# Other rates for the conditioning loads, three more steps before the transposes of the convolution rows, and a later request of norm rows in a two-layer decoder trunk

## The chip, the cores and the metric

The kernel runs on one core of one Trainium2 chip. The metric is device time in microseconds (us) of one execution, as the median of several runs. A core has five engines that work side by side, each through its own queue in order: TensorE (PE, matmuls and transposes), VectorE (DVE), ScalarE (ACT), GpSimd (POOL), and SyncE (SP), which here only issues DMA transfers. An instruction waits in its queue until what it needs is done, and everything behind it in that queue waits too.

## The reference

Two layers, one sequence of 256 tokens of width 2048. Each layer has a token mixer (forgetting attention in the first, sliding-window attention in the second) and a gated ConvFFN of inner width 5632. Every sub-layer is wrapped by a modulation and a norm whose six vectors come from the conditioning vector c:

```
c_act = jax.nn.silu(c)
for i in range(DEPTH):
    mod = c_act @ ada_w[i] + ada_b[i]
    sh1, sc1, g1, sh2, sc2, g2 = jnp.split(mod[:, None, :], 6, axis=-1)
    h = x * (1.0 + sc1) + sh1
    y = mixer(h)
    x = layer_norm(DEEPNORM_ALPHA * x + (1.0 + g1) * y, ln_mix_g[i], ln_mix_b[i])
    h = x * (1.0 + sc2) + sh2
    y = conv_ffn(h, ffn_w_up[i], ffn_conv_w[i], ffn_conv_b[i], ffn_w_down[i])
    x = layer_norm(DEEPNORM_ALPHA * x + (1.0 + g2) * y, ln_ffn_g[i], ln_ffn_b[i])
return x
```

All weights are f32. `ada_w` alone is two matrices of 2048 x 12288.

## The kernel before

**Weights and steps.** Every projection streams its weight in tiles of 256 rows by 512 columns (0.524 MB). `stream` asks for a tile on SP's queue (L261), ACT rounds it to a high part `wh` (L264), DVE subtracts to get the low part `wl` (L275), and PE multiplies high by high, high by low and low by high, so that the product has nearly the precision of f32. Four buffers each hold `wh` and `wl`; ten hold the loaded tiles. One consumed weight tile is one **step**: after it, `tick` runs some of the background work. The tokens are held on PE in the down and output projections (sums `xs`), the weights in the up projections (sums `ws`).

**Conditioning.** A vector (l, v) of `mod` (l the layer, v from 0 to 5: shift, scale, gate of the mixer, then of the ConvFFN) is a sum over 2048 rows of `ada_w`. `ada_vector` loads it in 32 tiles of 0.524 MB (L387, `wa`), and DVE adds each one, times an element of silu(c), to an accumulator `acc` (L393; the first by L391). There is one accumulator. For a shift or scale, PE then turns it in 16 transposes (L431), ACT sums the columns (L435) and DVE adds the bias (L417); a gate goes through four matmuls with ones (L403), after its bias came by a load on POOL's queue (L381). The vectors come in the order of `ada_list` (L363). How fast: each step adds `rate` to a debt, and each whole unit of debt runs one piece, mostly one load with its product (`ada_tick`, L461). When a scale (l, 4) is done, the generator holds until the next norm (L440). If a vector is needed and not there, `ada_need` (L467) runs the missing pieces at once. The rates are set stage by stage with numbers written into the program.

**Norms between sub-layers.** `between` (L1143) stands between two sub-layers: it asks for shift and scale, lets PE spin on a few dummy matmuls, normalises (`normalise`, L647 on ACT for the first 128 tokens, L649 on DVE for the others), transposes x on PE (L488) and applies the merged scale and shift (L681 to L683, then `mod_pair`, L498 to L503). x itself is still to be multiplied by the norm's weights for the next residual. That is background work: `affine` loads four tiles of norm rows on SP (L656) and runs two DVE operations for each of eight blocks of x (L667, L668), one block a step.

**Other background work.** `columns` (L142) turns the convolution weights from rows into columns: POOL requests the rows (L162, L163), a step later PE transposes them (L167), another step later DVE copies them to `ccol` (L169). It does this for both layers, one after the other. The rows take one of four buffers that are shared with sums of query and key parts and other short-lived tiles. In the second mixer `pair` runs the softmax of two heads over several steps.

**Order.** The engines' order comes from a scheduler that may move instructions past each other where data allow it, except those pinned to the program's order (`pin(..., True)`), among them the products L393 and the operations of `affine`. So a change of one number can move neighbours too.

Of the kernel before, what the change touches and what calls it, by code (L numbers as in the profile page):

```python
# [41 lines left out]
def hybrid_trunk(ctx: ExitStack, tc: tile.TileContext, a: dict, out: bass.AP):  # L42
# [99 lines left out]
    def columns():  # L142

        r = ttile("rows").rearrange("p (a b) -> p a b", b=P)
        for l in range(1, DEPTH):
            nc.gpsimd.dma_start(r[:NADA, l, :], adab[l])
        for q, nm in enumerate(("ln_mix_g", "ln_mix_b", "ln_ffn_g", "ln_ffn_b")):
            nc.gpsimd.dma_start(r[q * 32:(q + 1) * 32, 0, :], a[nm].rearrange("l (r p) -> (l r) p", p=P))
        yield
        for l in range(1, DEPTH):  # L150
            pt = bank()
            nc.tensor.transpose(pt[:, :NADA], r[:NADA, l, :], ident[:NADA, :NADA])
            yield
            nc.vector.tensor_copy(acol[:, l, :], pt[:, :NADA])
        pt = bank()
        nc.tensor.transpose(pt[:, :P], r[:, 0, :], ident)
        yield
        nc.vector.tensor_copy(lcol.rearrange("p a b c -> p (a b c)"), pt[:, :P])
        for l in range(DEPTH):
            r = ttile("rows").rearrange("p (a b) -> p a b", b=P)  # L160
            for j in range(CW):
                nc.gpsimd.dma_start(r[:NF, j, :], a["ffn_conv_w"][l, j].rearrange("(r p) -> r p", p=P))  # L162
            nc.gpsimd.dma_start(r[:NF, CW, :], a["ffn_conv_b"][l].rearrange("(r p) -> r p", p=P))  # L163
            yield
            pt = bank()
            for j in range(CW + 1):
                nc.tensor.transpose(pt[:, j * NF:(j + 1) * NF], r[:NF, j, :], ident[:NF, :NF])  # L167
            yield
            nc.vector.tensor_copy(ccol[:, l].rearrange("p a b -> p (a b)"), pt[:, :(CW + 1) * NF])  # L169
# [165 lines left out]
    def later(gens, lag=1):  # L335

        bg["wait"].extend((g, lag) for g in gens)
# [313 lines left out]
    def ln_rows(name, l):  # L651
        gb, bb = [], []
        for c in range(0, D, D // 2):
            for b, nm in ((gb, "_g"), (bb, "_b")):
                w = wtile("ln")
                nc.sync.dma_start(w.rearrange("p a f -> p (a f)"), a[name + nm][l, c:c + D // 2].partition_broadcast(P))  # L656
                b += [w[:, 0, :], w[:, 1, :]]
        return gb, bb

    def affine(name, l):  # L660

        gb, bb = ln_rows(name, l)
        yield
        for d in range(D // 512):
            c = slice(d * 512, (d + 1) * 512)
            for t in range(NT):
                pin(nc.vector.scalar_tensor_tensor(x[:, t, c], x[:, t, c], ALPHA, gb[d], op0=ALU.mult, op1=ALU.mult))  # L667
                pin(nc.vector.scalar_tensor_tensor(x[:, t, c], bb[d], ALPHA, x[:, t, c], op0=ALU.mult, op1=ALU.add))  # L668
                yield
# [70 lines left out]
    def out_proj(oT, full, w_o, l):  # L740
        def stat(kc, t):
            while kc not in full:
                step()
            return oT[kc][0][:, t * P:(t + 1) * P], oT[kc][1][:, t * P:(t + 1) * P]

        ps = {d: x_banks() for d in range(2)}

        def part(d, ks):
            use = x_mm_end(ps[d], stat, KC, 2) if d == D // WB - 1 else                 lambda kc, h, l_: x_mm(ps[d], kc, h, l_, stat, KC - 1)
            stream(w_o, 0, d * WB, ks, use)  # L750

        for i, ks in enumerate((range(0, 8), range(8, 12))):
            then(lambda i=i: ada.update(rate=(1.3, 0.3)[l]))
            for d in range(2):
                part(d, list(ks))
        then(lambda: (ada_need(l, 2), ada.update(rate=(1.3, 0.6)[l])))
        for d in range(D // WB):
            if d < 2:
                part(d, list(range(12, KC)))
            else:  # L760
                ps[d] = x_banks()
                part(d, list(range(KC)))
            then(lambda d=d: defer(residual(ps[d], d, gates[l, 2], True)), d == D // WB - 1)
        then(lambda: (flush(), ada.update(gate_free=True)), True)
# [204 lines left out]
    def swa(l, j):  # L969
# [94 lines left out]
        ps = x_stationary(w_in, KOFF, 0, KC, hstat)  # L1064
        for t in range(NT):
            then(lambda t=t, ps=ps: defer(evac_kv(t, ps[t])))
        then(lambda: (ada.update(rate=0.8), bg.update(gap=2)))
        for g in range(SKV):
            if g == 1:
                then(lambda: ada.update(rate=0.3))  # L1070
            ps = x_stationary(w_in, g * WB, 0, KC, hstat)
            then(lambda g=g, ps=ps: defer(evac_q(g, ps)))
        out_proj(oT, full, w_o, l)
# [2 lines left out]
    def conv_ffn(l):  # L1076
        w_up, w_dn = a["ffn_w_up"][l], a["ffn_w_down"][l]
        NB = DFF // WB
        cw = lambda j, f: ccol[:, l, j, f:f + 1]

        def conv(pf, f):
            u = tp.tile([P, S], F32, tag="u", bufs=3, name="u")
            nc.scalar.activation(u, pf, AF.Identity, bias=cw(CW, f), scale=cw(2, f))  # L1083
            nc.vector.scalar_tensor_tensor(u[:, 1:], pf[:, :S - 1], cw(1, f), u[:, 1:],  # L1084
                                           op0=ALU.mult, op1=ALU.add)
            nc.vector.scalar_tensor_tensor(u[:, 2:], pf[:, :S - 2], cw(0, f), u[:, 2:],  # L1086
                                           op0=ALU.mult, op1=ALU.add)
            return u

        def evac(ps, f0, then):  # L1090
            u = None
            for f in range(5):
                v = conv(ps[f // 2][:, f % 2, :], f0 + f) if f < 4 else None
                if u is not None:
                    then(f - 1, u)
                u = v
                yield
                yield

        def silu(sil):  # L1100
            def f_(f, u):
                nc.scalar.activation(sil[f // 2][:, (f % 2) * S:(f % 2 + 1) * S], u, AF.Silu)
            return f_

        def gated(sil, gT):
            def f_(f, u):
                nc.vector.tensor_tensor(u, u, sil[f // 2][:, (f % 2) * S:(f % 2 + 1) * S], op=ALU.mult)
                g = gtile("gT")
                split(g[:, 0, :], g[:, 1, :], u)
                gT.append(g)  # L1110
            return f_

        sbs = [(0, 6), (6, NB)]
        for si, (b0, b1) in enumerate(sbs):
            gT = []
            then(lambda: ada.update(rate=(0.64, 0.4)[l]))
            for b in range(b0, b1):
                ps = w_stationary(w_up, b * WB)
                sil = [ttile("sil") for _ in range(2)]
                then(lambda ps=ps, b=b, sil=sil: defer(evac(ps, b * 4, silu(sil))))  # L1120
                ps = w_stationary(w_up, DFF + b * WB)
                then(lambda ps=ps, b=b, sil=sil, gT=gT: defer(evac(ps, DFF // P + b * 4, gated(sil, gT))))

            def stat(kc, t, gT=gT):
                while kc >= len(gT):
                    run_post()
                return gT[kc][:, 0, t * P:(t + 1) * P], gT[kc][:, 1, t * P:(t + 1) * P]

            def ready(si=si):
                if si == 0:  # L1130
                    drain()
                ada_need(l, 5)
                ada["rate"] = (0.85, 0.4)[l]

            then(ready)
            for d in range(D // WB):
                ps = x_stationary(w_dn, d * WB, b0 * 4, (b1 - b0) * 4, stat, (2, 4)[l] if si > 0 and d == D // WB - 1 else 0)
                then(lambda ps=ps, d=d, si=si: defer(residual(ps, d, gates[l, 5], si == len(sbs) - 1)),
                     si > 0 and d == D // WB - 1)
        then(lambda: (flush(), ada.update(gate_free=True)), True)  # L1140


    def between(l, v, g, b, name, ll):  # L1143

        ada_need(l, v)
        ada_need(l, v + 1)
        place(20 if v else 56)
        o = bank("spin")
        release()
        spin(o, 3)  # L1150
        modulate(*merged(l, v, g, b, ll), normalise, o)
        behind[0] = 2
        later([affine(name, ll)])

    for l in range(DEPTH):
        if l > 0:
            then(lambda l=l: (between(l, 0, 2, 3, "ln_ffn", l - 1), ada.update(rate=.3)), True)
            swa(l, l // 2)
        else:
            fox(l, l // 2)  # L1160
        then(lambda l=l: between(l, 3, 0, 1, "ln_mix", l), True)
        conv_ffn(l)
# [36 lines left out]
```

## Time and profile before

| what | us |
|---|---|
| median of 3 runs | 2226.65 |
| lowest and highest of them | 2225.01 and 2227.9 |
| the profiled execution, its own time | 2226.14 |
| its span from the first to the last instruction | 2224.4 |
| PE busy within the span | 2168.7 |
| DVE busy | 1785.4 |
| ACT busy | 1152.5 |

In the profile's rows a group of instructions stands as: line, engine, operation, output<-inputs, size, count; then busy time, mean of one in ns, and idle time of the engine just before, with what ended it. In the timeline a row begins with the start in us from the span's beginning and the duration; brackets hold the idle time before it and what was waited for. `PEld` is PE's weight load, which runs beside its matmuls. In the view by windows each row is a stretch of time with its length, then each engine's busy time with the number of instructions, the granted share of PE's clock, the share of time the DMA engines were busy, and GB/s.

### The profile page before, as it was taken

The numbers are of one execution on the slowest core, as the hardware profiler recorded it, in microseconds if no ns is written. First come the engines' busy times: TensorE is split into PE (matmuls) and PEld (weight loads), VectorE is DVE, ScalarE is ACT, GpSimd is POOL, SyncE is SP. The second block draws the span as 40 slices with busy tenths as digits, with TensorE's granted clock in tenths as the row PEclk, the third lists the DMA queues.
The fourth block names the chain that finished last, engine by engine and source line by source line (L and its number), as shares of the span: only waits on it lengthen the run. The fifth ranks groups of instructions, "written<-read, shape, count | busy, mean of one in ns | idle before, by whom it ended". The sixth has DMA issues, their size and how long they took to land. (4 is left out here: it accounts for less than half of the span.)

```text
span 2224.4 us, 38328 instructions
## 1 busy us (share of the span) xinstructions
PE 2168.7 (97%) x14915; PEld 1973.9 (89%) x14915; DVE 1785.4 (80%) x2442; ACT 1152.5 (52%) x1825; POOL 19.9 (1%) x48
## 2 busy tenths in 40 slices
PE   6999999999999999999999999989999999999997
PEld 5999888889999888999987777779999888999986
DVE  6978999979979978798799877789888555666756
ACT  3435655555555543555634577555555533555532
POOL 0000000000000000000000000000000000000000
PEclk9999999999999999999999999999999999999998
DMA  9999999969979989799798755678888566666563
GB/s 337 382 359 345 348 358 321 330 222 331 345 250 313 327 300 348 263 307 320 251 344 304 257 181 163 208 272 291 281 270 267 183 195 191 198 191 197 192 194 109
DMA packets 274246, 602.98 MB, mean 271 GB/s; under 512 B 21062, under 2 KB 29960, under 8 KB 273552
## 3 DMA queue, kind: packets, MB, share of 16 engines
q1 hardware_dynamic: 273008, 595.85, 78.9%
q0 software_dynamic: 1056, 4.69, 0.6%
q8 instruction: 116, 1.90, 0.3%
q14 instruction: 66, 0.54, 0.1%
HBM read 598.37 MB, written 2.10 MB: 270 GB/s over the span
## 5 line engine op out<-in xcount | busy, mean ns | idle before, releaser
L264 ACT CAST wh<-w 128x1024 fp32r<-128x1024 f32 x728 | 765.4, 1053 | 810.1 <-PE ws L75 272.9
L275 DVE TENSOR_TENSOR wl<-w,wh 128x1024 fp32r<-128x1024 f32 x728 | 887.5, 1222 | 338.5 <-ACT wh L264 322.4
L75 PE MATMUL ws<-hH,wh 128*128 128x256 f32 x6656 | 1153.2, 278 | 4.6 <-ACT hH L84 2.1
L75 PEld LDWEIGHTS ws<-hH,wh 128*128 128x128 f32 x6656 | 1009.4, 189 | 12.5 <-issue 3.6
L75 PE MATMUL ws<-hH,wl 128*128 128x256 f32 x3328 | 916.5, 277 | 3.4 <-DVE wl L275 3.2
L75 PEld LDWEIGHTS ws<-hH,wl 128*128 128x128 f32 x3328 | 626.4, 189 | 4.9 <-DVE wl L275 4.8
L75 PE MATMUL xs<-wh,gT 128*128 128x512 f32 x1408 | 435.5, 389 | 0.0
L75 PEld LDWEIGHTS xs<-wh,gT 128*128 128x128 f32 x1408 | 264.3, 188 | 54.6
L75 PE MATMUL xs<-wl,gT 128*128 128x512 f32 x704 | 273.9, 389 | 0.0
L75 PE MATMUL xs<-wh,hH 128*128 128x512 f32 x704 | 236.8, 403 | 0.3 <-ACT wh L264 0.2
L393 DVE SCALAR_TENSOR_TENSOR acc<-wa,cact,acc 128x1024 f32<-128x1024 f32 x180 | 228.0, 1277 | 0.0
L393 DVE SCALAR_TENSOR_TENSOR acc<-wa,cactp,acc 128x1024 f32<-128x1024 f32 x128 | 162.4, 1277 | 0.0
L75 PEld LDWEIGHTS xs<-wh,hH 128*128 128x128 f32 x704 | 131.3, 189 | 29.9 <-issue 0.9
L75 PEld LDWEIGHTS xs<-wl,gT 128*128 128x128 f32 x704 | 132.2, 188 | 27.4
L75 PE MATMUL xs<-wl,hH 128*128 128x512 f32 x352 | 139.1, 396 | 2.2 <-DVE wl L275 2.2
L1083 ACT ACTIVATE u<-ws,ccol 128x256 f32<-128x256 f32 x176 | 96.7, 562 | 58.7 <-PE ws L75 44.4
L75 PE MATMUL xs<-wh,oT 128*128 128x512 f32 x384 | 124.9, 395 | 0.0
L1084 DVE SCALAR_TENSOR_TENSOR u<-ws,ccol,u 128x255 f32<-128x255 f32 x176 | 82.5, 477 | 18.0 <-ACT u L1083 17.8
L75 PEld LDWEIGHTS xs<-wh,oT 128*128 128x128 f32 x384 | 72.0, 188 | 15.8 <-DVE oT L85 0.3
L1086 DVE SCALAR_TENSOR_TENSOR u<-ws,ccol,u 128x254 f32<-128x254 f32 x176 | 83.0, 477 | 2.1
L75 PEld LDWEIGHTS xs<-wl,hH 128*128 128x128 f32 x352 | 66.5, 189 | 18.1 <-DVE wl L275 4.5
L568 DVE SCALAR_TENSOR_TENSOR oacc<-wo,cact,oacc 128x1024 f32<-128x1024 f32 (+1 forms) x68 | 73.4, 1079 | 8.6 <-DMA wo<-in_ada_w_dram 7.4
(215 smaller groups left out, 1265.9 us busy)
## 6 DMA issues: line engine op xcount, KB each, us to landing
w<-in_ffn_w_up_dram SPq DMA_DIRECT2D x352, 512.0 KB, 4.8
wa<-in_ada_w_dram SPq DMA_DIRECT2D x320, 512.0 KB, 5.7
w<-in_ffn_w_down_dram SPq DMA_DIRECT2D x176, 512.0 KB, 4.8
w<-in_fox_w_in_dram SPq DMA_DIRECT2D x96, 512.0 KB, 7.0
wo<-in_ada_w_dram SPq DMA_DIRECT2D x48, 512.0 KB, 9.4
w<-in_swa_w_in_dram SPq DMA_DIRECT2D x40, 512.0 KB, 4.7
w<-in_fox_w_o_dram SPq DMA_DIRECT2D x32, 512.0 KB, 6.3
w<-in_swa_w_o_dram SPq DMA_DIRECT2D x32, 512.0 KB, 4.4
```

The source lines that it names most:

```text
L75: return nc.tensor.matmul(o, lhsT, rhs, start=start, stop=stop, **kw)
L264: pin(nc.scalar.copy(h, w), False)
L275: pin(nc.vector.tensor_tensor(l, w, f32(h), op=ALU.subtract), behind[0] > 0)
L393: pin(nc.vector.scalar_tensor_tensor(ac, wo, (cactp if row else cact)[:, k:k + 1], ac, op0=ALU.mult, op1=ALU.add), True)
L568: nc.vector.scalar_tensor_tensor(acc, w[:, k], cact[:, kc:kc + 1], acc, op0=ALU.mult, op1=ALU.add)
L1083: nc.scalar.activation(u, pf, AF.Identity, bias=cw(CW, f), scale=cw(2, f))
L1084: nc.vector.scalar_tensor_tensor(u[:, 1:], pf[:, :S - 1], cw(1, f), u[:, 1:], op0=ALU.mult, op1=ALU.add)
L1086: nc.vector.scalar_tensor_tensor(u[:, 2:], pf[:, :S - 2], cw(0, f), u[:, 2:], op0=ALU.mult, op1=ALU.add)
```

## The change

It changes three things:

- conditioning rates: first ConvFFN, down projections 0.85 to 0.95; second layer: first norm and key/value projection 0.3 to 0.2, first query block 0.8 to 0.6, other query blocks 0.3 to 0.65, output projection 0.3 to 0.65 and from the third part on 0.6 to 0.75
- the background generator `columns` makes four yields in place of one between the request of the convolution rows and their transposes
- `affine` takes a delay in steps: 7 at the norm between the layers, 0 at the norms inside a layer, as before

Nothing is computed otherwise, and the loads, products and matmuls are as many as before. Lines behind the two insertions have numbers higher by 1 (from 165 on) or by 3 (from 662 on).

```
@@ -161,7 +161,8 @@
             for j in range(CW):
                 nc.gpsimd.dma_start(r[:NF, j, :], a["ffn_conv_w"][l, j].rearrange("(r p) -> r p", p=P))
             nc.gpsimd.dma_start(r[:NF, CW, :], a["ffn_conv_b"][l].rearrange("(r p) -> r p", p=P))
-            yield
+            for _ in range(4):
+                yield
             pt = bank()
@@ -657,8 +658,10 @@
-    def affine(name, l):
-
+    def affine(name, l, delay):
+
+        for _ in range(delay):
+            yield
         gb, bb = ln_rows(name, l)
         yield
@@ -750,10 +753,10 @@
-            then(lambda i=i: ada.update(rate=(1.3, 0.3)[l]))
+            then(lambda i=i: ada.update(rate=(1.3, 0.65)[l]))
             for d in range(2):
                 part(d, list(ks))
-        then(lambda: (ada_need(l, 2), ada.update(rate=(1.3, 0.6)[l])))
+        then(lambda: (ada_need(l, 2), ada.update(rate=(1.3, 0.75)[l])))
@@ -1064,10 +1067,10 @@
-        then(lambda: (ada.update(rate=0.8), bg.update(gap=2)))
+        then(lambda: (ada.update(rate=0.6), bg.update(gap=2)))
         for g in range(SKV):
             if g == 1:
-                then(lambda: ada.update(rate=0.3))
+                then(lambda: ada.update(rate=0.65))
@@ -1130,7 +1133,7 @@
-                ada["rate"] = (0.85, 0.4)[l]
+                ada["rate"] = (0.95, 0.4)[l]
@@ -1150,11 +1153,11 @@
-        later([affine(name, ll)])
+        later([affine(name, ll, 0 if v else 7)])
...
-            then(lambda l=l: (between(l, 0, 2, 3, "ln_ffn", l - 1), ada.update(rate=.3)), True)
+            then(lambda l=l: (between(l, 0, 2, 3, "ln_ffn", l - 1), ada.update(rate=.2)), True)
```

The numbers say little about where instructions now stand, so three places of the built order follow.

The first is DVE's queue at the last inner norm, between the second mixer and the second ConvFFN: the end of the last residual (L631 to L636), then the norm. Before:

```order
L631 BN_STATS stats<-x 128x6
L634 BN_AGGR mv<-stats 128x2
L636 TENSOR_SCALAR mv<-mv 128x1
L393 SCALAR_TENSOR_TENSOR acc<-wa,cact,acc 128x1024 x5
L649 TENSOR_SCALAR x<-x,mv,rs 128x512 x4
L417 SCALAR_TENSOR_TENSOR cv<-tot,acol 128x16
L681 TENSOR_TENSOR G<-cv,lcol 128x16
L682 TENSOR_TENSOR B<-cv,lcol 128x16
L683 TENSOR_TENSOR B<-B,cv 128x16
L499 TENSOR_SCALAR t<-sm,G,B 128x256 x2
```

After the change the same place reads:

```order
L632 BN_STATS stats<-x 128x6
L635 BN_AGGR mv<-stats 128x2
L637 TENSOR_SCALAR mv<-mv 128x1
L650 TENSOR_SCALAR x<-x,mv,rs 128x512 x4
L500 TENSOR_SCALAR t<-sm,G,B 128x256 x2
L501 TENSOR_TENSOR hH<-t,hH 128x256 x2
```

The five products of vector (1,4) and the four small operations that make its merged columns have left this place for the output projection ahead of it.

The second is PE's queue at the same norm, from the last matmuls of the output projection to the first transposes of x. Before:

```order
L75 MATMUL xs<-wh,hH 128x512 x2
L75 MATMUL xs<-wl,hH 128x512
L75 MATMUL xs<-wh,hH 128x512
L431 MATMUL sm<-ident,acc 128x128 x16
L75 MATMUL spin<-mask,ident 128x384 x3
L488 MATMUL sm<-ident,x 128x128 x8
```

With the change, where the second of four groups of such transposes stands inside the output projection (its sums go over oT and hH, the attention's result):

```order
L75 MATMUL xs<-wh,hH 128x512 x2
L75 MATMUL xs<-wl,hH 128x512
L75 MATMUL xs<-wh,hH 128x512
L432 MATMUL sm<-ident,acc 128x128 x4
L75 MATMUL xs<-wh,oT 128x512
L75 MATMUL xs<-wl,oT 128x512
```

The 16 transposes of the accumulator no longer stand between the mixer and the norm; they come in fours, between weight tiles.

The third is PE's queue in the first mixer, where the convolution rows of the first layer are turned (L167, L168 after; S is a head's scores). Before:

```order
L75 MATMUL ws<-hH,wh 128x256 x2
L75 MATMUL ws<-hH,wl 128x256
L167 MATMUL sm<-ident,rows 128x88 x3
L75 MATMUL ws<-hH,wh 128x256
L167 MATMUL sm<-ident,rows 128x88
```

After:

```order
L75 MATMUL ws<-hH,wh 128x256 x2
L75 MATMUL ws<-hH,wl 128x256
L168 MATMUL sm<-ident,rows 128x88 x4
L75 MATMUL S<-Bm,A 128x128
L75 MATMUL S<-qh 128x128
L75 MATMUL S<-ql,qh 128x128
```

They stand 88 matmuls further back and in one piece, ahead of a head's scores.

## The prediction

> **What bounds the kernel now.** I read the page's busy table first, then the waits of TensorE, then the three norms between sub-layers in the view by windows, and last the timeline of the one norm that stands out.
>
> ```profile
> span 2224.4 us, 38328 instructions
> PE 2168.7 (97%) x14915; PEld 1973.9 (89%) x14915; DVE 1785.4 (80%) x2442; ACT 1152.5 (52%) x1825; POOL 19.9 (1%) x48
> ```
>
> TensorE (PE) is busy for 2168.7 of 2224.4 us, so at most 55.7 us of the span are gaps. No rate changes the number of its matmuls. The change can only move gaps, so the question is which gaps it touches. The next view shows three stretches, each from the last matmul of one sub-layer to the first of the next; columns are busy time of PE, weight loads, VectorE (DVE), ScalarE (ACT), GpSimd (POOL), then granted clock, DMA share and GB/s.
>
> ```profile
> 470.46:476.28 5.82, 4.47 (x20) 2.65 (x19) 4.85 (x13) 4.47 (x8) 1.12 (x2) 1.00 0.00 0
> 1208.68:1214.51 5.83, 4.49 (x21) 2.65 (x19) 4.93 (x13) 4.52 (x8) 1.11 (x2) 1.00 0.21 84
> 1468.54:1484.98 16.44, 8.93 (x36) 6.62 (x35) 12.10 (x23) 10.49 (x42) 2.58 (x3) 0.69 0.64 228
> ```
>
> The first two norms take 5.82 and 5.83 us. The third, the last inner norm, takes 16.44 us, and there the granted clock is 0.69 instead of 1.00. The timeline says why:
>
> ```profile
> 1468.54 0.39 PE L75 MATMUL xs<-wh,hH 128*128 128x512 f32 x1
> 1476.44 3.67 PE L431 MATMUL sm<-ident,acc 128*128 128x128 f32 x16 [7.51 <-DVE acc L393]
> 1479.90 3.37 PE L75 MATMUL spin<-mask,ident 128*128 128x384 f32 x6
> 1483.11 1.04 PE L488 MATMUL sm<-ident,x 128*128 128x128 f32 x8
> 1484.98 0.69 PE L75 MATMUL ws<-hH,wh 128*128 128x256 f32 x2
> ```
>
> ```profile
> 1471.52 6.06 DVE L393 SCALAR_TENSOR_TENSOR acc<-wa,cact,acc 128x1024 f32<-128x1024 f32 x5
> 1477.49 1.91 DVE L649 TENSOR_SCALAR x<-x,mv,rs 128x512 f32<-128x512 f32 x4
> 1482.69 0.18 DVE L417 SCALAR_TENSOR_TENSOR cv<-tot,acol 128x16 f32<-128x16 f32 x1 [3.28 <-ACT sm L435]
> ```
>
> The scale vector that this norm needs, (1,4), isn't finished. Its last five products stand in DVE's queue ahead of the normalising of the second token tile; PE waits 7.51 us for them, then turns the sums in 16 transposes, ACT adds these up, and only then come the norm's own transposes (L488) and the next matmul.
>
> **The change part by part.**
>
> *The last norm.* The order after the change has all 32 loads of (1,4) inside the second mixer; its transposes stand in four groups of 4 within the output projection, and its column (L417 before) is computed two weight tiles ahead of the final residual. What is left between the last matmul of the mixer and the first of the ConvFFN is, row by row, what the first layer has at the same place, 5.82 us. So 16.44 - 5.82 = 10.6 us go. Bounds: the second norm, 5.83, gives the same to 0.01 us, so I keep 10.6 with no range of its own.
>
> The 16 transposes are not saved, they are paid elsewhere. At the full clock eight of the same size (L488) take 1.04 us above, 0.13 us each: 16 x 0.13 = 2.1 us. The upper bound is the 3.67 us of their own row at the reduced clock; I take 2.1, since they will stand in a busy stretch. They wait for DVE's last product; DVE runs ahead of PE there (below), so I add no wait. GpSimd's load of the bias for (1,5) now stands ahead of this norm's two powers on its queue (L637 before). It waits for those transposes, which end several weight tiles before the norm, so the powers don't wait for it.
>
> *Convolution rows.* POOL requests them, PE transposes them one step later and finds them missing (timeline, then the landing times of these tiles, then the first reader of the columns):
>
> ```profile
> 203.23 1.57 POOL L162 DMA_DIRECT2D rows<-in_ffn_conv_w_dram  x3 [2.82 <-DVE ze L810]
> 206.85 0.52 POOL L163 DMA_DIRECT2D rows<-in_ffn_conv_b_dram  x1
> 208.32 0.29 PE L167 MATMUL sm<-ident,rows 88*128 88x88 f32 x1 [0.36 <-DMA rows<-in_ffn_conv_w_dram]
> 209.90 0.57 PE L167 MATMUL sm<-ident,rows 88*128 88x88 f32 x2 [1.29 <-DMA rows<-in_ffn_conv_w_dram]
> 210.75 0.52 DVE L169 COPY ccol<-sm 128x352 f32<-128x352 f32 x1 [2.53 <-PE sm L167]
> ```
>
> ```profile
> DMA to landing us min/median/max: 1.7/5.7/6.3
> ```
>
> ```profile
> L1083 ACT ACTIVATE u<-ws,ccol x176: 546/565/570, 501.5 to 2108.2; 128x256 f32<-128x256 f32 x176
> ```
>
> The wait is 0.36 + 1.29 = 1.65 us, and DVE stands 2.53 us behind it. A step is one weight tile, 12 matmuls in a projection with the tokens held still:
>
> ```profile
> 1205.06 0.39 PE L75 MATMUL xs<-wl,gT 128*128 128x512 f32 x1
> 1207.78 0.39 PE L75 MATMUL xs<-wl,gT 128*128 128x512 f32 x1
> ```
>
> That is 2.72 us, so three more steps put the transposes 8.2 us later, near 216.5; the last request, at 206.85, has landed by 213.2 even at the slowest 6.3. The wait goes. The gain is 1.65 us; it could be 2.5 if what DVE stands is regained too. Against it, the rows hold one of four shared buffers for three steps more, and the sums of query and key parts use the same four; a sum that comes late could cost as much as the wait did. Range: 2.5 gained to 1.7 lost; I take the 1.65. The columns themselves are first read at 501.5, so their own lateness is covered by the whole attention.
>
> *First ConvFFN, rate 0.85 to 0.95.* In the order of loads on SP's queue the first down projection carries 39 conditioning loads instead of 34, the second up projection 38 instead of 41, the second down projection 30 instead of 31. Each load brings one DVE product. The rows are the two groups of operations (busy us, mean ns of one, idle before), the stretch of the second down projection, and the longest wait of ACT in it.
>
> ```profile
> L275 DVE TENSOR_TENSOR wl<-w,wh 128x1024 fp32r<-128x1024 f32 x728 | 887.5, 1222 | 338.5 <-ACT wh L264 322.4 <-DMA wa<-in_ada_w_dram 3.8 <-DMA w<-in_ffn_w_up_dram 3.2
> L393 DVE SCALAR_TENSOR_TENSOR acc<-wa,cact,acc 128x1024 f32<-128x1024 f32 x180 | 228.0, 1277 | 0.0
> 1095.00:1210.00 115.00, 115.00 (x531) 95.86 (x530) 105.21 (x113) 48.45 (x51) 0.56 (x1) 1.00 0.95 339
> ACT wh L264 <- PE xs L75: 60.9, 38, 3.0
> ```
>
> The tightest place is the second down projection, 1095 to 1210: DVE idles 115 - 105.2 = 9.8 us. In DVE's order the first 32 of its 40 steps now hold 29 products instead of 24: 5 x 1.28 = 6.4 us more, against 32/42 of that idle time, 7.5 us. It fits, barely. What covers a late residual is that ACT, which feeds DVE, waits 60.9 us of this stretch for PE to free the four split buffers: the split weights lie ready and PE is the one behind. If none of the idle time could be used, 6.4 us less a lead of two steps, 5.4, would leave 1.0 us. Range 0 to 1.0; I take 0.2.
>
> Those 32 steps bring 61 tiles:
>
> ```profile
> wa<-in_ada_w_dram SPq DMA_DIRECT2D x320, 512.0 KB, 5.7
> 100.00:125.00 25.00, 24.82 (x180) 22.65 (x179) 21.01 (x22) 10.39 (x13) 0.00 (x0) 1.00 1.05 387
> 1175.00:1200.00 25.00, 25.00 (x112) 20.71 (x111) 24.16 (x24) 9.51 (x9) 0.00 (x0) 1.00 1.01 373
> ```
>
> 61 x 0.524 MB = 32.0 MB in 32 x 2.72 = 87 us is 367 GB/s. The trace moved 373 in this very projection without a gap on PE, and 387 near the kernel's start, so I add nothing.
>
> The Trainium skill speaks against this: "DMA: Bandwidth & Descriptors", section Specifications, gives an HBM limit of about 358 GB/s per core, by which the 32.0 MB would take an estimated 89.4 us, 2.4 more than PE needs. The 387 GB/s of the row above exceeds that limit, so here the measurement decides against it.
>
> *Second mixer: rates 0.2, 0.6, 0.65, 0.75 and the late affine.* Sixteen loads instead of 12 stand in its input projection and 16 instead of 15 in its output projection. On SP's queue the four loads of norm rows (L656) move from behind 8 of the mixer's weight tiles to behind 15, past seven of them, which come that much earlier; the 16 DVE operations on x move with them. In DVE's order the second and third query block (1260.0 to 1312.7 before) gain 6 conditioning products and 13 affine operations.
>
> ```profile
> 1260.00:1312.70 52.70, 52.70 (x293) 41.90 (x292) 40.90 (x105) 34.72 (x75) 0.00 (x0) 1.00 0.75 241
> 1312.70:1415.80 103.10, 102.92 (x619) 77.31 (x618) 75.36 (x230) 76.04 (x204) 0.00 (x0) 1.00 0.52 162
> L667 DVE SCALAR_TENSOR_TENSOR x<-x,ln 128x512 f32<-128x512 f32 x8 | 5.5, 685 | 0.0
> ACT wh L264 <- PE xs L75: 11.0, 9, 1.7
> ```
>
> That is 6 x 1.28 + 13 x 0.69 = 16.6 us against 52.7 - 40.9 = 11.8 us idle: 4.8 us over. Behind it in DVE's queue stand the softmax steps of the first heads, for which PE waits. The cover is the lead: ACT still waits for PE in this stretch (11.0 us from 1260 to 1416), so splits are ready two to three steps ahead, 5.4 to 8.2 us. From 1312.7 on DVE has 27.7 us idle and gets 7 products more, 9.0 us, so the backlog goes there. Range 0 to 4.8; I take 0.8, nearer to the end at which the lead holds. DMA is at 241 and 162 GB/s, far below the 373 above.
>
> *After the norm.* PE's long wait also let the other engines fill their buffers:
>
> ```profile
> 476.30:526.30 50.00, 49.19 (x423) 48.44 (x422) 48.76 (x67) 29.41 (x40) 0.00 (x0) 1.00 0.77 254
> 1485.00:1535.00 50.00, 49.88 (x435) 49.55 (x434) 48.31 (x67) 28.97 (x40) 0.00 (x0) 1.00 0.75 247
> ```
>
> After the long norm PE is busy 49.88 of 50 us, after the first layer's 49.19. Without the pause I expect the latter, 0.7 us lost.
>
> **The sum**: -10.6 + 2.1 - 1.65 + 0.2 + 0.8 + 0.7 = -8.45 us, so a span of 2215.95. The profiled execution took 2226.1 us, 1.7 more than its span; the median of the runs shown is 2226.65, 0.5 above it. On the median the forecast is 2226.65 - 8.45 = 2218.2 us.
>
> **Rivals.**
>
> *The lead runs out in the second mixer.* The 4.8 us are paid in full and a little stays from the first ConvFFN (1.0): 2218.2 + 4.0 + 0.8 = 2223.0 us. For it: DVE's own idle time doesn't cover the added work. Against: from 1260 to 1416 PE's weight loads wait for DVE 0.2 us at the longest.
>
> ```profile
> PEld S L75 <- DVE nm L695: 1.5, 8, 0.2
> ```
>
> *The added work isn't covered at all, and the kernel gets slower.* If the heads' softmax chain, not DVE's total, sets the pace in the second mixer, every product ahead of it counts: 16.6 + 9.0 = 25.6 us in place of my 0.8. It decides from 8.45 + 0.8 = 9.25 us on, 36% of that work. All of it would give 2218.2 + 24.8 = 2243.0, half of it 2230.2. Against it: PE is busy 102.92 of 103.10 us in that stretch.
>
> *The wait only moves.* The transposes now stand in PE's queue inside the output projection; if the products come late, PE stands there as it did at the norm, 7.5 us: 2225.7 us. Against it: of 8.7 us that such transposes wait in all, 7.5 are those of the last norm; the five other vectors, turned inside projections, share 1.2.
>
> ```profile
> PE sm L431 <- DVE acc L393: 8.7, 2, 7.5
> ```
>
> *Transfers bind in the second down projection.* From 1095 to 1210 the queues move 339 GB/s at a share of 0.95, which is 357 at a share of 1. If that were the ceiling, the 32.0 MB would take 89.6 us, 2.6 more than PE needs: 2220.8. Against it stand 373 and 387.
>
> *More is gained.* Full 2.5 for the rows and no loss elsewhere: 2218.2 - 0.85 - 1.7 = 2215.65.
>
> **How the numbers follow.** Forecast and its near surroundings (2216 to 2222) 0.63; more gained 0.08; transfers 0.04; lead runs out 0.10; the wait moves 0.07; slower 0.08. A measurement of this kernel can't tell less than about 0.2%, 4.5 us, from no change. Faster (under 2222.2): 0.63 + 0.08 + 0.04 + half of 0.10 = 0.80; same: 0.05 + 0.07 = 0.12; slower 0.08. The range leaves 2 in 10 outside: 2214.5, just below the larger gain, to 2224, past the lead that runs out.
>
> **What would show it.** The stretch from the mixer's last matmul to the ConvFFN's first is about 5.8 us with a clock of 1.00 (now 16.44 and 0.69); L393 has no wait of 7.5 us behind it; the waits of PE on the rows are gone near 208; the windows of the second mixer stay as busy on PE as now. I am wrong if PE waits for DVE inside the second mixer or at the moved transposes, or if gaps open in the second down projection.

## The result and the profile after

The changed kernel takes 2218.61 us (median of 6 runs, 2217.09 to 2223.02), the kernel before 2227.28 in runs on the same chip (median of 6, 2224.81 to 2229.03). The ratio is 0.9966, 95% interval 0.9953 to 0.9979. The forecast was 2218.2. A second comparison, the last pair of the experiments below, gave 2219.57 against 2225.14, ratio 0.9974 (0.9964 to 0.9983).

The total came out almost exactly. That doesn't mean that its terms did, so the stages are taken one by one. First the page of the changed kernel.

```profile
span 2221.3 us, 38316 instructions
PE 2170.6 (98%) x14915; PEld 1976.7 (89%) x14915; DVE 1784.0 (80%) x2442; ACT 1151.8 (52%) x1825; POOL 19.0 (1%) x48
```

This profiled execution took 2223.02 us, the slowest of its six runs, 4.4 above their median, whereas the profiled execution before lay 0.5 below the median of the runs shown there. So the two spans differ by 3.1 us only and the medians by 8.7. To see why, I cut both traces at the last matmul of each sub-layer and at the first of the next, and the first sub-layer once more after its first 40 steps:

| stretch, us | before | after | difference | forecast |
|---|---|---|---|---|
| start to step 40 | 170.51 | 173.74 | +3.2 | 0 |
| rest of the first mixer (the convolution rows) | 299.95 | 297.91 | -2.0 | -1.65 |
| first norm | 5.82 | 5.82 | 0.0 | 0 |
| first ConvFFN | 732.40 | 732.60 | +0.2 | +0.2 |
| second norm | 5.83 | 5.82 | 0.0 | 0 |
| second mixer | 254.03 | 260.06 | +6.0 | +2.1 + 0.8 |
| last inner norm | 16.44 | 5.89 | -10.55 | -10.6 |
| second ConvFFN | 725.14 | 725.18 | 0.0 | +0.7 |

Without the first row the stages sum to -6.3 us. The first row is no effect of the change: to step 40 the two programs run the same work in the same order. The same windows by engine, before, after, and of a second profiled execution of the changed kernel (the last of the runs below), show what differs; the clock stands behind POOL's busy time.

```profile
0.00:170.51 170.51, 148.88 (x984) 137.61 (x984) 132.83 (x149) 67.54 (x90) 6.24 (x25) 0.95 1.02 360
```

```profile
0.00:173.74 173.74, 151.95 (x984) 141.73 (x984) 133.12 (x148) 67.76 (x90) 6.24 (x25) 0.93 1.00 346
```

```profile
0.00:169.81 169.81, 148.71 (x983) 137.54 (x984) 132.88 (x148) 67.75 (x90) 6.27 (x25) 0.95 1.02 362
```

The same 984 matmuls, with a granted clock of 0.93 in one execution of the changed kernel and 0.95 in the other. Differences of 3 us between two profiled spans of this kernel therefore say nothing by themselves; stages from step 40 on can be compared. Whole runs scatter in the same way: of the ten runs of the second comparison the three at a mean clock of 0.995 took 2216.95 to 2217.31 us, the one at 0.992 took 2223.07.

**The last norm** now reads like the others (view by windows, then PE's timeline):

```profile
471.65:477.48 5.83, 4.48 (x21) 2.65 (x19) 4.86 (x13) 4.48 (x8) 1.12 (x2) 1.00 0.00 0
1210.08:1215.90 5.82, 4.48 (x20) 2.65 (x19) 4.92 (x13) 4.51 (x8) 1.11 (x2) 1.00 0.00 0
1475.96:1481.85 5.89, 4.48 (x21) 2.66 (x19) 4.92 (x13) 4.52 (x8) 1.11 (x2) 1.00 0.00 1
```

```profile
1476.19 2.10 PE L75 MATMUL spin<-mask,ident 128*128 128x384 f32 x6
1478.78 0.66 PE L489 MATMUL sm<-ident,x 128*128 128x128 f32 x4 [0.49 <-ACT x L648]
1480.35 0.66 PE L489 MATMUL sm<-ident,x 128*128 128x128 f32 x4 [0.92 <-DVE x L650]
1481.85 0.70 PE L75 MATMUL ws<-hH,wh 128*128 128x256 f32 x2
```

No transposes of the accumulator, no wait over a microsecond, clock 1.00. In the waits of PE over the whole span the wait of 7.5 us on L393 (now L394) is gone, and what is left of 8.7 us is one short one:

```profile
PE sm L432 <- DVE acc L394: 1.2, 1, 1.2
```

It stands at 439.98 us in the first mixer, where the kernel before waited as long (1.15 us at 438.81). The moved transposes don't wait.

**The convolution rows** are turned in one piece, without a wait (PE's timeline):

```profile
221.28 0.47 PE L168 MATMUL sm<-ident,rows 88*128 88x88 f32 x4
```

**The second mixer** is where forecast and result disagree. The whole stage, before, then after:

```profile
1214.51:1468.54 254.03, 253.85 (x1353) 198.20 (x1352) 204.63 (x453) 158.96 (x343) 0.00 (x0) 1.00 0.66 213
```

```profile
1215.90:1475.96 260.06, 257.57 (x1370) 200.87 (x1368) 210.30 (x462) 164.44 (x375) 0.58 (x1) 1.00 0.68 223
```

PE stood idle for 0.18 us of this stage (254.03 - 253.85) and now for 2.49; its busy time grew by 3.7 with 16 transposes more (the ends of matmuls are modelled, so part of a stall may count as busy). The loss lies among the heads. From step 416 to step 448 the heads run beside the last two query blocks and the start of the output projection; this stretch took, before and after:

```profile
1290.52:1424.80 134.28, 134.10 (x802) 101.47 (x801) 98.62 (x290) 96.44 (x252) 0.00 (x0) 1.00 0.53 165
```

```profile
1291.73:1430.27 138.54, 136.05 (x802) 102.45 (x801) 112.48 (x309) 97.86 (x255) 0.00 (x0) 1.00 0.65 209
```

4.3 of the 6.0 us are in it. DVE is busy 13.9 us more there, and yet has 26 us idle: its total isn't the limit. How its work reaches PE can be read in one timeline (rows of DVE, ACT and PE; `pr` are a pair's probabilities, `es` and `ss` its sums, `T` and `pT` the turned probabilities, `oT` the heads' output, `S` the next scores):

```profile
1381.88 0.16 DVE L1041 TENSOR_TENSOR es<-nm,sink 128x4 f32<-128x4 f32 x1
1381.96 1.28 DVE L394 SCALAR_TENSOR_TENSOR acc<-wa,cact,acc 128x1024 f32<-128x1024 f32 x1
...
1383.35 0.18 DVE L1045 RECIPROCAL ss<-ss 128x4 f32<-128x4 f32 x1
...
1383.62 0.91 ACT L1052 ACTIVATE pr<-pr,ss 128x256 f32<-128x256 f32 x2 [1.34 <-DVE ss L1045]
...
1384.43 1.03 ACT L265 CAST wh<-w 128x1024 fp32r<-128x1024 f32 x1
...
1385.50 1.23 DVE L276 TENSOR_TENSOR wl<-w,wh 128x1024 fp32r<-128x1024 f32 x1 [1.46 <-ACT wh L265]
...
1386.64 0.42 DVE L85 TENSOR_TENSOR oT<-o,oT 128x256 fp32r<-128x256 f32 x1
...
1387.12 0.33 PE L75 MATMUL S<-kT,qT 64*128 64x128 f32 x1 [0.40 <-DVE oT L85]
...
1387.79 0.44 PE L75 MATMUL S<-kT,qT 64*128 64x128 f32 x3 [0.34 <-DVE nm L698]
```

The kernel before has no product at the same place:

```profile
1378.92 0.18 DVE L1042 RECIPROCAL ss<-ss 128x4 f32<-128x4 f32 x1
1379.19 0.91 ACT L1049 ACTIVATE pr<-pr,ss 128x256 f32<-128x256 f32 x2 [0.50 <-DVE ss L1042]
1381.08 1.23 DVE L275 TENSOR_TENSOR wl<-w,wh 128x1024 fp32r<-128x1024 f32 x1 [1.46 <-ACT wh L264]
```

A conditioning product of 1.28 us stands between two short operations of a softmax. ACT now waits 1.34 us for the reciprocal instead of 0.50, and what hangs on it moves back by about as much: its next cast, DVE's split of that cast with the softmax steps of the next pair queued behind it, and PE's scores. DVE's wait of 1.46 us for the cast was there before too, so it isn't the loss; the loss is the shift. Against the kernel before, PE's matmuls come 3.5 us late ahead of this place and 4.4 us late behind it. DVE's idle time is in large part the other side of this waiting, 18.2 of the 26 us end with a cast of ACT, so only some of it is room.

### The profile page after: what moved, and what is told of

Same layout as the page of the kernel before. It is cut to its first block, busy times and chain, and to the rows that moved or that the text cites. A ratio compares the mean times of both kernels' runs of the same rounds, so it can differ in the third digit from the quotient of the medians.

```text
span 2221.3 us, 38316 instructions
## 1 busy us (share of the span) xinstructions
PE 2170.6 (98%) x14915; PEld 1976.7 (89%) x14915; DVE 1784.0 (80%) x2442; ACT 1151.8 (52%) x1825; POOL 19.0 (1%) x48
## 5 line engine op out<-in xcount | busy, mean ns | idle before, releaser
L394 DVE SCALAR_TENSOR_TENSOR acc<-wa,cact,acc 128x1024 f32<-128x1024 f32 x180 | 228.4, 1278 | 0.0
L394 DVE SCALAR_TENSOR_TENSOR acc<-wa,cactp,acc 128x1024 f32<-128x1024 f32 x128 | 162.2, 1277 | 0.0
```

The source lines that it names most:

```text
L394: pin(nc.vector.scalar_tensor_tensor(ac, wo, (cactp if row else cact)[:, k:k + 1], ac, op0=ALU.mult, op1=ALU.add), True)
```

## The experiments

Each kernel was compared with the kernel before on the same chip. Beside the median, the table gives the second mixer of the profiled execution, of it the stretch from step 416 to 448, and how many conditioning products DVE started in that stretch.

| kernel | median us | ratio, 95% | second mixer | steps 416 to 448 | products |
|---|---|---|---|---|---|
| before (the one profiled) | 2225.14 to 2227.28 | 1 | 254.03 | 134.28 | 10 |
| changed | 2218.61 | 0.9966 (0.9953, 0.9979) | 260.06 | 138.54 | 21 |
| rows only | 2225.70 | 0.9989 (0.9980, 0.9999) | 254.00 | | |
| no delay | 2218.52 | 0.9966 (0.9954, 0.9978) | 257.87 | 136.32 | 20 |
| output projection alone | 2219.34 | 0.9972 (0.9962, 0.9982) | 259.54 | 133.52 | 13 |
| delay alone | 2228.04 | 1.0009 (1.0000, 1.0019) | 255.02 | 135.56 | 11 |
| early products | 2219.96 | 0.9977 (0.9968, 0.9987) | 261.65 | 138.68 | 14 |
| late products | 2216.15 | 0.9959 (0.9945, 0.9973) | 257.07 | 135.22 | 17 |
| early products and delay | 2223.66 | 0.9988 (0.9979, 0.9998) | 262.13 | 139.25 | 14 |
| ConvFFN rate back | 2219.04 | 0.9971 (0.9960, 0.9983) | 259.83 | 138.15 | 20 |
| late products again | 2216.89 | 0.9965 (0.9951, 0.9978) | 257.10 | 135.24 | 17 |
| changed again | 2219.57 | 0.9974 (0.9964, 0.9983) | 260.11 | 138.60 | 21 |

The stages repeat well: the changed kernel and the one with late products, profiled twice each, agree with themselves within 0.06 us in the last columns, while the medians, of five to ten runs that spread over some 3 to 6 us, moved by 0.7 and 1.0.

**Rows only.** The kernel before with the three added steps.

```
-            yield
+            for _ in range(4):
+                yield
             pt = bank()
```

> The kernel before with the three more steps for the convolution rows and nothing else. Theory: the wait of 1.65 us on the rows goes and the time is kept, so from the 40th to the 128th weight tile the first mixer takes about 2.2 us less than the 299.7 us of before, the mixer between norms two and three stays at 254.0 us and the last norm at 16.4 us; the whole is 2 us faster. Rival: the first mixer is bound by DVE and the transfers, the gain is eaten before the first norm, 0 us.

From step 40 to the end of the first mixer it took 297.8 us against 299.95 before, 2.2 less; the second mixer kept its 254.0, and the last norm is still long, 16.09 us (PE's timeline):

```profile
1477.99 3.68 PE L432 MATMUL sm<-ident,acc 128*128 128x128 f32 x16 [7.51 <-DVE acc L394]
```

The rows are worth 2.0 to 2.3 us by the stages, in all nine profiles with the added steps (297.65 to 297.91 us). By the runs they are worth 0.1% as a ratio, with medians only 0.1 us apart. They have no share in the norm.

The profile before doesn't show all that this wait can cost. Two kernels below keep the one step, and in both PE waited longer for the rows and the clock halved behind it. In the one with the delay alone (PE's timeline, then the window behind it):

```profile
212.30 0.30 PE L167 MATMUL sm<-ident,rows 88*128 88x88 f32 x1 [1.84 <-DMA rows<-in_ffn_conv_w_dram]
214.10:217.50 3.40, 3.40 (x18) 3.40 (x18) 3.40 (x4) 0.00 (x0) 0.00 (x0) 0.50 0.85 266
```

There the stretch from step 40 took 300.4 us, and 301.2 in the run with the output projection alone, against 299.95 in the profile before.

**Delay alone** is the kernel before with `affine`'s seven steps, **no delay** the changed kernel without them.

```
...
-        later([affine(name, ll)])
+        later([affine(name, ll, 0 if v else 7)])
```

> The kernel before with the affine's delay of 7 steps and nothing else. If the affine operations among the first heads cost the 4.1 us, the mixer takes 258 us in place of 254.0 and the whole is 4 us slower; if the added products do, the mixer stays at 254 to 255 us and the whole is the same. The last norm stays at 16.4 us in both.

```
-        later([affine(name, ll, 0 if v else 7)])
+        later([affine(name, ll, 0)])
```

> The changed kernel with the delay of the affine at 0 instead of 7 steps. Of the 6.0 us by which the second mixer grew (254.0 to 260.1), 1.9 are the moved transposes. Theory: the other 4.1 come from the 16 affine operations that now collide with the heads' softmax, so without the delay the mixer takes about 256 us and the whole is 4 us faster. Rival: they come from the added conditioning products between the heads, so the mixer stays at 259 to 260 us.

Alone, the delay lengthens the second mixer by 1.0 us. Taken out of the changed kernel, it shortens it by 2.2 (260.06 to 257.87), nearly all of it among the heads:

```profile
1291.12:1427.44 136.32, 134.49 (x801) 101.70 (x800) 110.09 (x302) 96.15 (x251) 0.00 (x0) 1.00 0.64 202
```

So the delay costs 1.0 us alone and 2.2 beside the added products. The theory gave it 4.1, its rival nothing; it came out between. How it costs time in this stretch isn't shown: in the changed kernel the delayed operations end at 1285.0, beside the first softmax steps and 6.7 us before the stretch begins. All that got shorter with the delay alone is the last norm, 15.54 us at a clock of 0.78 against 16.44 and 16.09 in two kernels without it; in the changed kernel the norm takes 5.9 with the delay or without. The medians, 2218.52 and 2218.61, don't show these 2 us; only the stages do.

**Output projection alone.** The rates of the kernel before, except in the output projection of the second layer, where enough products are run to complete the scale there.

```
-            then(lambda i=i: ada.update(rate=(1.3, 0.3)[l]))
+            then(lambda i=i: ada.update(rate=((1.3, 1.3)[i], (0.3, 0.8)[i])[l]))
...
-        then(lambda: (ada_need(l, 2), ada.update(rate=(1.3, 0.6)[l])))
+        then(lambda: (ada_need(l, 2), ada.update(rate=(1.3, 1.1)[l])))
```

> The kernel before with higher conditioning rates in the second output projection alone: 0.8 in its second part, 1.1 from its third part on; (1,4) is then complete ahead of the last norm, with no product added between the heads and no other part of the change. Theory: the norm falls from 16.4 to 5.9 us, the mixer grows from 254.0 by the 1.9 us of the transposes alone, the whole is 8.6 us faster than before. Rival: ten products in eight steps of the output projection make DVE late there, and the mixer grows by 4 us or more.

The norm takes 5.89 us here too. So the theory holds for the norm, and the gain at the norm needs only that the scale is complete; neither the rates of the first ConvFFN nor of the input projection, nor the delay, nor the rows. For the mixer the rival came true: it grew by 5.5 us. The heads lose nothing (133.52), but the output projection does. Ten products stand in eight of its steps (timeline, then windows around it):

```profile
1435.43 3.67 DVE L393 SCALAR_TENSOR_TENSOR acc<-wa,cact,acc 128x1024 f32<-128x1024 f32 x3
...
1437.93 0.38 SPq L261 DMA_DIRECT2D w<-in_swa_w_o_dram  x1
...
1439.01 1.22 DVE L275 TENSOR_TENSOR wl<-w,wh 128x1024 fp32r<-128x1024 f32 x1
1439.06 0.84 PE L75 MATMUL xs<-wh,oT 128*128 128x512 f32 x3
...
1441.26 1.04 ACT L264 CAST wh<-w 128x1024 fp32r<-128x1024 f32 x1 [3.44 <-DMA w<-in_swa_w_o_dram]
...
1442.36 0.50 PE L75 MATMUL xs<-wh,oT 128*128 128x512 f32 x1 [2.46 <-ACT wh L264]
```

```profile
1439.50:1443.00 3.50, 1.04 (x5) 0.56 (x4) 3.50 (x4) 1.04 (x1) 0.00 (x0) 1.00 0.90 310
1443.00:1446.50 3.50, 3.50 (x10) 2.76 (x9) 3.50 (x4) 0.00 (x0) 0.00 (x0) 0.52 1.02 359
```

Three products in a row hold DVE for 3.67 us; ACT waits 3.44 us for a weight tile, PE 2.46 for ACT, and the next 3.5 us run at a clock of 0.52. As I read it, the tile is late because SP's requests of weights stand in line with those of conditioning tiles, and both with DVE, which frees their buffers. Here the lead of two to three steps did run out.

**Early products** and **late products** are the changed kernel without the delay and with the second mixer's products dealt out differently; the former also ran with the delay. Rates in order: key/value projection, first query block, other query blocks, and the three parts of the output projection.

```
   changed         0.2  0.6  0.65 | 0.65 0.65 0.75
   early products  0.9  0.9  0.3  | 0.5  0.6  0.8
   late products   0.3  0.8  0.3  | 0.75 0.8  0.95
```

> The changed kernel without the affine's delay, and with the conditioning of the second mixer dealt out otherwise: 0.9 in the key/value projection and the first query block, 0.3 in the other query blocks, 0.5, 0.6 and 0.8 in the output projection. In DVE's order the three later query blocks (the heads) then hold 8 products instead of 16, the first query block 8 instead of none, the output projection 16 as before. Theory A (products among the heads cost because the softmax steps stand behind them in DVE's queue): the second mixer takes 254.0 + 1.9 for the transposes, so 256 to 256.5 us against 257.87 without the delay and 260.06 with it; the stretch of the last norm stays at 5.9; the median is 2216.5 to 2217.5. Theory B (all products are equal, wherever they stand in the mixer): 257.9 again, median 2218.5. Theory C (the first query block has no room for 8 products): 258 to 261, with the stalls there.

> The changed kernel without the affine's delay, with the rates 0.3, 0.8 and 0.3 of the kernel before up to the heads, and 0.75, 0.8 and 0.95 in the output projection. In DVE's order 9 products stand in the later query blocks (16 with the change), 21 in the output projection, 9 of them in its third block of eight steps. Theory A: few products among the heads and fewer in a bunch than the ten that left a stall of 2.6 us in the run with the output projection alone, so the second mixer takes 256 to 257 and the median 2216.5 to 2217.5. Theory B (all products are equal): 257.9 and 2218.5. Theory C (nine in eight steps already empty the split buffers): a stall of about 2 us on PE near 1435 to 1440, with the clock at half behind it, 259 to 260, median 2219 to 2220.

> As the run with the early products, with the affine's delay of seven steps back in: its eight operations pairs then stand in the second query block beside 3 products rather than 5. Theory A (the delay costs where its operations meet products ahead of softmax steps): 1.0 us, as the delay alone cost, to 1.5 us more than without it, so the second mixer takes 257 to 257.5. Theory B (the delay costs the same 2.2 us as in the changed kernel, whatever the products do): 258.2 to 258.7. Median 1 to 2 us above the run without the delay.

Late products came out close to theory A: 257.07 us, median 2216.15. Early products did not. They have fewer products among the heads than the changed kernel, 14 against 21, and take as long there, 138.68. The price isn't one per product. Most of it stands at one place (rows of DVE, ACT and PE, then a window):

```profile
1380.80 0.15 DVE L1044 TENSOR_TENSOR ss<-ss,es 128x4 f32<-128x4 f32 x1
1380.88 1.28 DVE L394 SCALAR_TENSOR_TENSOR acc<-wa,cact,acc 128x1024 f32<-128x1024 f32 x1
1382.07 0.17 DVE L1045 RECIPROCAL ss<-ss 128x4 f32<-128x4 f32 x1
...
1382.34 0.91 ACT L1052 ACTIVATE pr<-pr,ss 128x256 f32<-128x256 f32 x2 [1.73 <-DVE ss L1045]
...
1384.88 0.55 PE L729 MATMUL T<-ident,pr 128*128 128x128 f32 x3 [0.77 <-ACT pT L731]
1385.83 0.32 PE L75 MATMUL S<-kT,qT 64*128 64x128 f32 x1 [0.40 <-DVE oT L85]
1386.50 0.43 PE L75 MATMUL S<-kT,qT 64*128 64x128 f32 x3 [0.35 <-DVE nm L698]
```

```profile
1380.00:1392.50 12.50, 10.99 (x58) 7.95 (x58) 8.86 (x23) 7.91 (x23) 0.00 (x0) 0.86 0.58 170
```

A product between the sum and its reciprocal, where the output projection starts and the last heads are still due: over the three waits shown PE falls 1.7 us further behind the kernel before, and then the clock falls to half for 3.4 us (0.86 over this window), another 1.5. Together that is 3.3 of the 4.4 us that these heads take longer than before. The same place in the order elsewhere (the late products have one at 1365.9 us, and ACT waits 1.83 us for its reciprocal) cost PE nothing visible, so which pair has slack decides, and that I can't tell from the order. Ahead of the heads, from the mixer's start to step 416, the early products took 77.3 us against 76.0 before. The one wait of PE there over 0.1 us stands right behind the first query block:

```profile
1267.15 0.50 PE L75 MATMUL xs<-wl,hH 128*128 128x512 f32 x1 [0.87 <-DVE wl L276]
```

This is the stall that theory C named, but it is the smaller part; the whole, 261.65 us, is past its 258 to 261, and the larger loss lies among the heads.

With the delay on top the second mixer took 0.5 us more in the profiled execution, less than either theory said. The median rose by 3.7. The profiled execution was the fastest of its ten runs (2218.83 to 2226.26), and the slow ones had a lower clock: the three at a mean clock of 0.994 took 2218.83 to 2220.67 us, the five at 0.991 and 0.992 took 2224.18 to 2226.26. Without the delay the runs at 0.994 took 2218.41 to 2219.76. So most of the 3.7 us goes with the clock; whether the delay has a part in the lower clock stays open.

**ConvFFN rate back** is the changed kernel with 0.85 in the down projections of the first ConvFFN.

```
-                ada["rate"] = (0.95, 0.4)[l]
+                ada["rate"] = (0.85, 0.4)[l]
```

> The changed kernel with the first ConvFFN's down projections back at rate 0.85. Theory A (the rate costs nothing, since the first ConvFFN took 732.40 and 732.60 us with the one and the other): the first ConvFFN takes 732.3 to 732.6, the second mixer 260 as in the changed kernel, and the median stays at 2218.5. Theory B (the higher rate is what makes room in the second mixer for the products): with seven products more in its first steps the second mixer takes 262 or more, and the median rises by 2 us or more.

The first ConvFFN takes 732.36 us and the second mixer 259.83: theory A. This part of the change costs 0.2 us in its own stage, and no gain from it can be seen here.

**The two best side by side.** The intervals of the late products and of the changed kernel overlapped, so both ran once more, together.

> The kernel with the late products and without the affine's delay once more, beside the changed kernel on the same chip, since their intervals overlapped (0.9945 to 0.9973 and 0.9953 to 0.9979). Theory A (the three microseconds of the second mixer, 257.07 against 260.06, are there in every execution): its median lies 2 to 3 us below that of the changed kernel of this batch. Theory B (they are one execution's chance, as the kernel's opening is): the two medians lie within 1 us.

> The changed kernel once more, as the neighbour of the run with the late products: 2217.5 to 2219, the second mixer 259.5 to 260.5 and the first to third norm 5.8 to 5.9 us in its profiled execution; under theory A 2 to 3 us above the late products, under theory B within 1 us.

2216.89 against 2219.57, 2.7 us apart, with second mixers of 257.10 and 260.11: theory A. The heads of the late products, beside which the changed kernel's are 138.60:

```profile
1287.65:1422.89 135.24, 134.28 (x802) 101.47 (x800) 106.26 (x295) 96.71 (x249) 0.00 (x0) 1.00 0.61 190
```

The two intervals against the kernel before still overlap (0.9951 to 0.9978 and 0.9964 to 0.9983), but the stage differs by 3.0 us in both pairs of profiles. The changed kernel itself came 0.6 us above the 2217.5 to 2219 expected of it. The late products are the best version found.

## Why the prediction held, and which term did not

**The last norm: right.** Forecast -10.6, measured -10.55, with the clock of 1.00 named beforehand. The rates of the output projection alone reached the same 5.89 us, which shows the cause.

**The moved transposes: right.** 16 x 0.13 = 2.1 was forecast. In the kernels that have them the rest of the second mixer, outside steps 416 to 448, takes 121.5 to 121.9 us (changed, no delay, late products) against 119.75 before: 1.8 to 2.1. They stand between 1449.8 and 1463 us, and PE has no wait from 1430 us to the end of the mixer. So the rival "the wait only moves" is out.

**Convolution rows: right, somewhat small.** -1.65 was forecast, -2.0 to -2.3 measured against the profile before, between that and the bound of 2.5 with what DVE regains. The transposes came at 221.28, not near 216.5: 3.2 us of this are the slower opening, the other 1.6 come from steps longer than the 2.72 us that I took, as heads stand between weight tiles. That the clock halved behind this wait in two other kernels was no term of the sum. The shared buffers cost nothing that shows.

**First ConvFFN: right.** +0.2 forecast and measured, 0.0 with the old rate. In its tightest place, the first 87 us of the second down projection, DVE came close to its limit, 84 of 87 us, and PE had no gap, before and after:

```profile
1095.10:1182.10 87.00, 87.00 (x408) 72.90 (x407) 80.05 (x86) 37.10 (x41) 0.00 (x0) 1.00 0.94 328
```

```profile
1096.40:1183.40 87.00, 87.00 (x407) 72.58 (x406) 84.01 (x90) 36.94 (x41) 0.00 (x0) 1.00 0.98 352
```

The rival of bound transfers didn't come true: 352 GB/s moved without a wait of PE, under the 357 at which it would have bound. The limit of about 358 GB/s that the Trainium skill gives ("DMA: Bandwidth & Descriptors", Specifications) was not reached in these 87 us. The Trainium skill, on the same page under Bandwidth, gives this figure for each of two cores that stream together and 425 GB/s, measured in a large transfer, for one alone; the prediction left that out. This kernel runs on one core, and its opening moved 385 again (rows of the last section).

**Second mixer: the mis-sized term.** 0.8 us was forecast for added products and late affine, at the end of the range "at which the lead holds". Beside the transposes the stage lost about 4: 2.0 among the heads from the added products (136.32 - 134.28), 2.2 from the delay on top of them (138.54 - 136.32). The step that failed is the cover: I held the lead in split weights against DVE's added work. PE did not wait for weights among the heads; its longest wait was 0.8 us for `oT`, and the others, 0.3 to 0.4 us, stood at `S`, at `qp` and at the sums of `oT`: the chain of softmax and heads, for which no split weight lies ready. This was the mechanism of the rival that ends slower, "the heads' softmax chain, not DVE's total, sets the pace". It was real, but at 4 of the 25.6 us that it would cost if every product counted, below the 9.25 us from which it decides. Which products count was only read from timelines. "PE is busy 102.92 of 103.10 us" was no argument against it: that was the state without the added work.

**After the norm: wrong, nothing lost.** +0.7 was forecast because the first layer without the pause was busy 49.19 of 50 us. The same windows of the changed kernel:

```profile
477.50:527.50 50.00, 49.21 (x423) 48.48 (x422) 48.79 (x67) 29.39 (x40) 0.00 (x0) 1.00 0.76 254
1481.85:1531.85 50.00, 49.88 (x435) 49.53 (x434) 48.79 (x68) 29.78 (x41) 0.00 (x0) 1.00 0.74 244
```

PE is busy for 49.88 us without any long pause ahead of it. So the pause was not what made the second layer start full; the 0.7 us belong to the first layer, and why is open.

**Why the total was so near.** By the stages the change is worth -6.3 us, not -8.45: the mixer took 3.1 us more than forecast, and the rows (0.4) and the start of the last ConvFFN (0.7) gave back a third. The medians of the two comparisons differ by 8.7 and 5.6 us, on both sides of 6.3. The forecast of 2218.2 met the first to 0.4 us by luck, with the help of that scatter; against the second it is 1.4 low.

## What to carry to other kernels

Idle time of an engine is safe room for background work where nothing latency-bound runs through its queue. Beside independent streams, as in the down projection, work of 4 us fitted into 7 us of gaps. In a stage where short operations of two engines wait for each other, one operation of 1.28 us in the middle of the chain came back as lateness on the third in some places and cost nothing in others. Place such work ahead of or behind the chain, few at a time, and compare stages between profiles rather than spans.

## What the runs showed of the hardware

The granted clock of PE halved in places without a pause. In the profiled execution of the changed kernel, with PE busy all along:

```profile
112.00:122.00 10.00, 10.00 (x79) 9.43 (x77) 6.43 (x6) 4.21 (x5) 0.00 (x0) 1.00 1.05 385
122.00:129.00 7.00, 7.00 (x33) 6.70 (x34) 5.39 (x8) 2.23 (x3) 0.00 (x0) 0.51 1.05 382
```

In the profile before, the second of these windows has 52 matmuls at a clock of 1.00. Such a stretch of some 6.8 us at half speed costs 3.4 us, and the trace of each execution has several, of 6.8 or 3.4 us, in its first 170 us, not all at the same places. By that sum, one stretch more or less is what separates the openings of 170.51 and 173.74 us.

Between 175 us and the last 15 us, none of the twelve profiles has such a stretch without a pause of PE just before it or beside it, and short pauses were followed by one: 2.46 us in the run with the output projection alone (0.52 behind it), 1.84 with the delay alone (0.50 behind it), and three waits of 0.35 to 0.77 us in the early products. That the pause is the cause is read from this order alone; in the profile before, the waits of 0.36 and 1.29 us on the rows had no such stretch behind them. The Trainium skill, "TensorE: Matmul & The Clock Gate", in "HAM oscillation — how this bites in real kernels", gives as its rule that PE should have no idle gaps over about 3.4 us. Here the clock halved behind shorter ones and, at 122 us, behind none that the trace shows.
